# Hybrid encoder on one core: second softmax map in PSUM, query projections beside the first heads, last chunks by token tile

## The chip, the cores and the metric

The kernel runs on one core of one Trainium2 chip. The metric is device time in microseconds for one execution. A core has five engines with a queue of instructions each: TensorE (PE, matmuls, whose weight loads are counted apart as PEld), VectorE (DVE), ScalarE (ACT), GpSimd (POOL) and SyncE (SP), which here issues the DMAs. The engines run side by side and wait for each other by semaphores.

## The reference, cut to what matters

The reference is a bidirectional encoder with two layers on a sequence of 1024 tokens of width 1024, in float32. Each layer projects x to four groups of mixers (a convolution module, an S5 state-space layer, a short gated convolution, differential attention), concatenates the four results, projects them out, normalises, runs a SwiGLU feed-forward network of hidden width 2816 and normalises again. The change touches the attention and the end of the feed-forward network:

```python
def block(q_blk):
    s = jnp.einsum('bqhcd,bkhcd->cbhqk', q_blk, k).astype(jnp.float32)
    p = jax.nn.softmax(s, axis=-1)
    a = p[0] - lam * p[1]
    return jnp.einsum('bhqk,bkhe->bqhe', a.astype(v.dtype), v)

o = lax.map(block, qb).swapaxes(0, 1).reshape(bsz, seq, DA_HEADS, DA_VDIM)
of = of * lax.rsqrt(jnp.mean(of * of, axis=-1, keepdims=True) + LN_EPS)
...
mix = jnp.einsum('bse,ed->bsd', jnp.concatenate([y_a, y_b, y_c, y_d], axis=-1), w_out[l])
x = layer_norm(DEEPNORM_ALPHA * x + mix, ln1_g[l], ln1_b[l])
ff = jax.nn.silu(x @ w_ffn1[l]) * (x @ w_ffn3[l])
x = layer_norm(DEEPNORM_ALPHA * x + ff @ w_ffn2[l], ln2_g[l], ln2_b[l])
```

There are 4 heads with 2 maps each, 8 query blocks of 128 tokens, queries and keys of 32 elements and values of 64. lam is one learned number per layer.

## The kernel before, in words

Float32 matmuls are made of three float32r matmuls on operands split into a high and a low part (`mm3`, lines 554 to 558; `split`, 560).

**Order of the work.** The class `Trunk` describes the computation, but it issues nothing itself: a recorder (`Weaver`, line 112 on) takes down each operation with what it reads and writes. `schedule` (306) then orders all operations of an engine's queue by a list schedule: an operation's priority is its number in the recording plus a shift from the table `SHIFT`, which has an entry for each step and layer (`attn_k0` is step `attn_k` in layer 0); the table `PREF` shifts the choice of engine where an operation can run on more than one (`any2`, `any3`, `anyp`). `emit` (468) issues them. So every instruction of the program carries line 473 in the profile, and is told by the names of its tiles. Large SBUF tiles (`S`, 525) share 11 slots of 16 KB, handed on in the order in which tiles are first used. PSUM has three pools: `g` (line 540) and `b` (543) with two buffers of one bank each, `d` (546) with two buffers of two banks each.

**A layer.** `mixers_in` (1615) streams nine blocks of the input projection through a ring of two weight tiles (`win`), in the order that `in_blocks` (1608) gives; the last three are V, Q and K. `tok_gemm` (645) makes the projection of a pair of token blocks: 48 matmuls 128x256 into a tile `tg` in PSUM. `attn_k` (1256) stores K's projection in `probs` as a buffer, applies rope on POOL, stacks high and low parts (`stg`, on ACT and POOL) and transposes them on PE (`ktp`) into `kst`. `attn_q` (1249) does projection and rope for Q into `vq`. `attn_small` (1198) makes lambda, `load_out` (1368) loads and splits the output weights (`wout`).

**Attention.** `run` (1679) calls `attn_heads` (1293) for each of 8 query blocks j. For each of 4 heads and 2 maps, two matmuls 128x512 write a score tile `sc` (pool `d`), DVE takes the row maximum (into `asm`), ACT computes the exponential into `probs` with its row sum. Then, per head, DVE takes the reciprocals of both sums, scales the second (`asm<-asm,lam`) and combines the two maps (`probs<-probs,asm`). Eight transposes (`atp`) and copies (`aT`) follow, and per pair of heads 32 matmuls `po` with V. After the first pair, `q_stack` (1282) prepares the next block's queries (`qtp`). `attn_finish` (1339) normalises the block's heads and splits the block's four mixer results into `yhl`; `out_half` (1383) and `out_norm` (1395) project out the block before (`wo`) and normalise it in `xr`.

**Feed-forward network.** `token_operands` (1406) prepares the operands, `ffn_up` (1479) makes the two up projections by a scheme of seven products (`up`), whose gated results go to DRAM by way of `gst`. The down projection is again seven products m, each over 11 chunks: `down_prep` (1552) brings a chunk into the rings `aring` and `wring`, `down_unit` (1570) makes three matmuls for each of four token tiles, `down_out` (1578) adds the product into the result `r`. After the products m = 5 and m = 6, `layer_norm` (575) and, in layer 0, `to_xT` (609, transposes `xtp`) finish four token tiles each.

## Time and profile before

| | |
|---|---|
| median of 3 runs | 2503.61 us (2501.72 to 2503.86) |
| the profiled execution | 2499.38 us |
| its span, first to last instruction | 2497.6 us |
| mean granted TensorE clock | 0.961 |
| busy: PE, DVE, POOL, ACT | 92%, 71%, 39%, 32% |

The profiled execution is 1.8 us longer than its span, and 4.2 us shorter than the median. Busy shares are means over the whole program; the windows below give the same by stage. "PEclk" is the clock that TensorE was granted, 1.00 being full speed. A timeline row has the start in us, the duration, the operation with its output and inputs, how many of its kind stand in the row, and in brackets the engine's idle time before it with the operation that ended it. A row of a group has busy time in all, mean duration in ns, and the idle time before its members.

### The profile page before, as it was taken

The page shows a single profiled execution, that of the slowest core. Times are in us where ns is not written, and L with a number is a line of the kernel's source. Part 1 is how long each engine was busy: PE and PEld are TensorE (multiplying, and loading weights), DVE is VectorE, ACT ScalarE, POOL GpSimd, SP SyncE. Part 2 cuts the span into 40 slices and gives each one's busy share as a digit, 9 for nine tenths or more (in the row PEclk, how much of TensorE's full clock was granted, in tenths as well). Part 3 has the DMA queues.
Part 4 walks back from the last instruction along what each step waited for, and adds up shares of the span by engine and source line. Part 5 has one row for each costly group of instructions (what it writes and reads, how often), then busy time and mean ns, then how long its engine had stood idle before and what let it go on. Part 6 is the DMA issues. An engine that isn't in the chain of part 4 may idle for free. (4 is left out here: it accounts for less than half of the span.)

```text
span 2497.6 us, 35091 instructions
## 1 busy us (share of the span) xinstructions
PE 2307.0 (92%) x13300; PEld 1911.4 (77%) x13300; DVE 1785.5 (71%) x2909; ACT 806.2 (32%) x1387; POOL 982.9 (39%) x876
## 2 busy tenths in 40 slices
PE   8999959888999999999989999699989999998996
PEld 7779847666888888778777788477778888886784
DVE  6587578886343443777881975999886777778988
ACT  2412246543222222332334132455433223222220
POOL 2104264535999899433430226444310000002414
PEclk9999959998999999999999999699999999999998
DMA  5223121112232333843332222111223323447332
GB/s 157 71 50 98 31 87 54 56 56 85 81 110 89 118 99 126 310 153 95 118 123 51 62 80 65 60 56 65 77 74 107 117 80 118 152 156 274 93 96 103
DMA packets 213953, 252.92 MB, mean 101 GB/s; under 512 B 57043, under 2 KB 143641, under 8 KB 213529
## 3 DMA queue, kind: packets, MB, share of 16 engines
q1 hardware_dynamic: 213784, 250.67, 31.4%
q8 instruction: 106, 1.74, 0.3%
q14 instruction: 63, 0.51, 0.1%
HBM read 183.82 MB, written 66.81 MB: 100 GB/s over the span
## 5 line engine op out<-in xcount | busy, mean ns | idle before, releaser
L473 PE MATMUL up<-xT,wring 128*128 128x512 f32 x2112 | 486.5, 389 | 1.0 <-POOL wring L473 1.0
L473 PEld LDWEIGHTS up<-xT,wring 128*128 128x128 f32 x2112 | 396.2, 188 | 84.3 <-POOL wring L473 2.1
L473 PE MATMUL dn<-wring,aring 128*128 128x512 f32 x1848 | 432.8, 396 | 25.8 <-DVE aring L473 11.1
L473 PEld LDWEIGHTS dn<-wring,aring 128*128 128x128 f32 x1848 | 351.0, 191 | 105.9 <-DVE aring L473 14.0
L473 PE MATMUL up<-xB,wring 128*128 128x512 f32 x1584 | 368.7, 390 | 0.0
L473 PEld LDWEIGHTS up<-xB,wring 128*128 128x128 f32 x1584 | 298.4, 189 | 62.0
L473 PE MATMUL cg<-xh,win 128*128 128x512 f32 x640 | 209.5, 397 | 4.2 <-DVE conv L473 4.2
L473 PE MATMUL tg<-win,xh 128*128 128x256 f32 x1024 | 194.4, 290 | 1.6 <-ACT s5u L473 0.7
L473 PE MATMUL wo<-wout,yhl 128*128 128x512 f32 x768 | 194.8, 401 | 0.0
L473 ACT ACTIVATE probs<-sc,asm 128x1024 f32<-128x1024 f32 x128 | 143.2, 1120 | 109.2 <-DVE asm L473 103.5
L473 ACT CAST wring<-upraw 128x512 fp32r<-128x512 f32 x164 | 101.9, 621 | 232.0 <-PE up L473 175.9
L473 DVE TENSOR_REDUCE asm<-sc 128x1 f32<-128x1024 f32 x128 | 155.3, 1217 | 25.3 <-PE sc L473 24.9
L473 PEld LDWEIGHTS tg<-win,xh 128*128 128x128 f32 x1024 | 163.6, 196 | 3.6 <-ACT s5u L473 0.9
L473 PEld LDWEIGHTS wo<-wout,yhl 128*128 128x128 f32 x768 | 143.3, 191 | 29.6 <-POOL yhl L473 0.3
L473 DVE TENSOR_TENSOR aring<-araw,aring 128x512 fp32r<-128x512 f32 x152 | 126.9, 842 | 45.8 <-ACT aring L473 42.8
L473 POOL TENSOR_TENSOR upraw<-upraw 128x512 f32<-128x512 f32 x32 | 42.4, 1324 | 292.4 <-ACT wring L473 292.4
L473 POOL TENSOR_TENSOR wring<-upraw,wring 128x512 fp32r<-128x512 f32 x110 | 148.0, 1346 | 6.1 <-ACT wring L473 4.2
L473 PE MATMUL tg<-win,xl 128*128 128x256 f32 x512 | 149.0, 292 | 1.0 <-DVE xl L473 1.0
L473 PEld LDWEIGHTS cg<-xh,win 128*128 128x128 f32 x640 | 120.2, 188 | 31.9 <-DVE conv L473 4.3
L473 ACT CAST aring<-araw 128x512 fp32r<-128x512 f32 x115 | 71.1, 622 | 206.5 <-PE dn L473 168.2
L473 DVE TENSOR_TENSOR tw<-tu,up 128x512 f32<-128x512 f32 x66 | 45.3, 686 | 123.6 <-PE up L473 119.5
L473 PE MATMUL sc<-kst,stg 128*128 128x512 f32 x256 | 96.9, 473 | 31.3 <-ACT probs L473 30.8
(263 smaller groups left out, 3986.4 us busy)
## 6 DMA issues: line engine op xcount, KB each, us to landing
upraw<-in_w_ffn_dram SPq DMA_DIRECT2D x88, 512.0 KB, 3.7
araw<-a_scr SPq DMA_DIRECT2D x154, 256.0 KB, 2.9
a_scr<-gst SPq DMA_DIRECT2D x22, 1536.0 KB, 6.0
...
```

Of the source, the lines that this page charges most:

```text
L473: getattr(e, method)(*args, **kwargs)
```

## The change

Five things are changed.

1. In `attn_heads` the exponentials of a head's second map are written back into the score tile in PSUM; `probs` now has one row per head (four in all) for the first map. Only the second sum's reciprocal is taken per head; its scaling by the first sum and lambda is on POOL; the combination on DVE reads the second map from PSUM. `attn_finish` takes the four other reciprocals at once.
2. The input blocks come in the order V, K, Q. `mixers_in` projects K and the first two token blocks of Q; the other three projections of Q are recorded after the heads of block 0. The tiles `yhl`, `wout` and `xr` are made after them.
3. The operand ring of the down projection is made before the tiles of its weights. In layer 0 this gives it the slot of the second-last `gst` tile in place of that of an up operand (`xB11`); in layer 1 it has the second-last `gst` tile's slot before and after.
4. The last four chunks of the last product (m = 6) are done token tile by token tile, the 12 matmuls of a tile in one go, each tile followed by its sums, its normalisation and, in layer 0, its transposes.
5. All entries of `SHIFT` and `PREF` are new, two of them for example:

```diff
-            "attn_k0": -385, "attn_k1": -165, "attn_q0": 5594, "attn_q1": -532, "attn_small1": 2064,
+            "attn_k0": -598, "attn_k1": 1732, "attn_q0": 484, "attn_q1": -1392, "attn_small0": 5048,
```

The rest of the diff (a class attribute `COMB`, an empty tuple, goes as well):

```diff
@@ -1256,11 +1254,11 @@
     def attn_k(self, xT, w, jp):
         nc = self.nc
         if jp == 0:
-            self.PA = self.S([P, 2, 2, SEQ], F32, "probs")
+            self.PA = self.S([P, 4, SEQ], F32, "probs")
             self.stg = self.S([P, 4, 1024], F32R, "stg")
             self.K = [self.S([P, 4, SEQ], F32R, f"kst{i}") for i in range(2)]
         ps = self.tok_gemm(xT, w, jp)
-        kk = self.PA[:, jp // 2, jp % 2, 0:512].rearrange("p (j n) -> p j n", j=2)
+        kk = self.PA[:, jp, 0:512].rearrange("p (j n) -> p j n", j=2)
         nc.scalar.copy(kk, ps)
         self.rope_pair(kk, jp)
         for i2 in range(2):
@@ -1276,7 +1274,6 @@
 
     def attn_alloc(self):
         self.yhl = self.S([P, 2, 2, KT, P], F32R, "yhl")
-        self.xr = self.S([P, 2, 2, D], F32, "xr")
 
     @step
     def q_stack(self, j):
@@ -1302,7 +1299,8 @@
         for hp in range(2):
             aTs = []
             for h in (2 * hp, 2 * hp + 1):
-                pb = self.PA[:, h % 2]
+                pb = self.PA[:, h]
+
                 for c in range(2):
                     m = 2 * h + c
                     sc = self.d((P, SEQ), "sc")
@@ -1310,20 +1308,16 @@
                         nc.tensor.matmul(sc[:, hf * 512:hf * 512 + 512], lhsT=qst[:, m * P:m * P + P],
                                          rhs=self.K[m // 4][:, m % 4, hf * 512:hf * 512 + 512], start=True, stop=True)
                     v.tensor_reduce(sm[:, m:m + 1], sc, axis=AX.X, op=ALU.max, negate=True)
-                    nc.scalar.activation(pb[:, c, :], sc, AF.Exp, bias=sm[:, m:m + 1], accum_out=sm[:, 8 + m:9 + m])
-                rc = sm[:, 16 + 2 * h:18 + 2 * h]
-                v.reciprocal(rc, sm[:, 8 + 2 * h:10 + 2 * h])
-                v.scalar_tensor_tensor(rc[:, 1:2], rc[:, 1:2], sm[:, 8 + 2 * h:9 + 2 * h], self.neglam, op0=ALU.mult, op1=ALU.mult)
-                if h in self.COMB:
-                    nc.scalar.activation(pb[:, 1, :], pb[:, 1, :], AF.Copy, scale=rc[:, 1:2])
-                    nc.gpsimd.tensor_tensor(pb[:, 0, :], pb[:, 0, :], pb[:, 1, :], op=ALU.add)
-                else:
-                    v.scalar_tensor_tensor(pb[:, 0, :], pb[:, 1, :], rc[:, 1:2], pb[:, 0, :], op0=ALU.mult, op1=ALU.add)
+                    nc.scalar.activation(sc if c else pb, sc, AF.Exp, bias=sm[:, m:m + 1], accum_out=sm[:, 8 + m:9 + m])
+                rc = sm[:, 16 + h:17 + h]
+                v.reciprocal(rc, sm[:, 9 + 2 * h:10 + 2 * h])
+                nc.gpsimd.tensor_scalar(rc, rc, sm[:, 8 + 2 * h:9 + 2 * h], self.neglam, op0=ALU.mult, op1=ALU.mult)
+                v.scalar_tensor_tensor(pb, sc, rc, pb, op0=ALU.mult, op1=ALU.add)
...
@@ -1349,7 +1343,8 @@
         ot = self.b((P, 4, 64), "ot")
         for i in range(2):
             self.tr(ot[:, 2 * i:2 * i + 2, :].rearrange("p h e -> p (h e)"), wf[:, i * P:i * P + P])
-        v.tensor_tensor(w, ot, sm[:, 16:24:2].unsqueeze(2).to_broadcast([P, 4, 64]), op=ALU.mult)
+        v.reciprocal(sm[:, 20:24], sm[:, 8:16:2])
+        v.tensor_tensor(w, ot, sm[:, 20:24].unsqueeze(2).to_broadcast([P, 4, 64]), op=ALU.mult)
@@ -1567,21 +1562,22 @@
         self.split(w(b), sb[:, 0], sb[:, 1])
 
     @step
-    def down_unit(self, n, ps):
-        c = n % (NHID // 2)
-        sa, sb = self.aring[:, n % 4], self.bring[:, n % 4]
-        for i in range(4):
+    def down_unit(self, ns, ps, tiles):
+        for i in tiles:
             s = slice(i * P, i * P + P)
-            self.mm3(ps[i], sa[:, 0, s], sa[:, 1, s], sb[:, 0], sb[:, 1], c == 0, c == NHID // 2 - 1)
-
-    @step
-    def down_out(self, m, ps, r, u):
+            for n in ns:
+                c = n % (NHID // 2)
+                sa, sb = self.aring[:, n % 4], self.bring[:, n % 4]
+                self.mm3(ps[i], sa[:, 0, s], sa[:, 1, s], sb[:, 0], sb[:, 1], c == 0, c == NHID // 2 - 1)
+
+    @step
+    def down_out(self, m, ps, r, u, tiles=range(4)):
 
         nc = self.nc
         v = nc.vector
         add = lambda o, x, y=None: v.tensor_tensor(o, o if y is None else y, x, op=ALU.add)
         axpy = lambda o, x: v.scalar_tensor_tensor(o, o, ALPHA, x, op0=ALU.mult, op1=ALU.add)
-        for i in range(4):
+        for i in tiles:
@@ -1606,7 +1602,7 @@
 
 
     def in_blocks(self):
-        return [OFF_S5, 0, GW, OFF_SC + GW, OFF_SC + 2 * GW, OFF_SC, OFF_DA + 2 * GW, OFF_DA, OFF_DA + GW]
+        return [OFF_S5, 0, GW, OFF_SC + GW, OFF_SC + 2 * GW, OFF_SC, OFF_DA + 2 * GW, OFF_DA + GW, OFF_DA]
 
     def in_ring(self, l):
         self.win = [self.S([P, 2, KT, GW], F32R, "win") for _ in range(2)]
@@ -1672,9 +1668,9 @@
             self.attn_v(xT, w(6), jp)
         nxt(7)
         for jp in range(4):
-            self.attn_q(xT, w(7), jp)
-        for jp in range(4):
-            self.attn_k(xT, w(8), jp)
+            self.attn_k(xT, w(7), jp)
+        self.attn_q(xT, w(8), 0)
+        return w(8)
 
     def run(self):
         nc, t = self.nc, self.t
@@ -1697,15 +1693,19 @@
             self.to_xT(j, x0[j // 4][:, j % 4, :], xT)
         for l in range(DEPTH):
             self.layer = l
-            self.mixers_in(l, xT, yT)
+            wq = self.mixers_in(l, xT, yT)
             self.attn_small(l)
-            self.load_out(l)
-            self.attn_alloc()
             g1, b1 = self.gain_rows(t["ln1_g"], t["ln1_b"], l, "ln1")
             xsrc = xin if l == 0 else x2d
             hls = {}
             for j in range(NJ):
                 sm_o = self.attn_heads(l, j)
+                if j == 0:
+                    for jp in range(1, 4):
+                        self.attn_q(xT, wq, jp)
+                    self.attn_alloc()
+                    self.load_out(l)
+                    self.xr = self.S([P, 2, 2, D], F32, "xr")
                 if 0 < j < NJ - 1:
                     hl = hls.pop(j - 1)
                     self.out_half(j - 1, hl, xsrc, 0)
@@ -1741,9 +1741,9 @@
+            self.aring, self.bring = self.S([P, 4, 2, 512], F32R, "aring"), self.wring
             self.w2_tiles((2, 3, 0, 4, 5))
             r = [self.S([P, 4, D], F32, "r") for _ in range(2)]
-            self.aring, self.bring = self.S([P, 4, 2, 512], F32R, "aring"), self.wring
@@ -1770,7 +1770,17 @@
-                self.down_unit(n, ps)
+                if m == 6 and c >= NC - 4:
+
+                    if c == NC - 1:
+                        for i in range(4):
+                            self.down_unit(range(n - 3, n + 1), ps, (i,))
+                            self.down_out(m, ps, rr, us, (i,))
+                            self.layer_norm(rj(tile_of[i]), g2, b2, (out if l + 1 == DEPTH else x2d)[tile_of[i]], 2)
+                            if l + 1 < DEPTH:
+                                self.to_xT(tile_of[i], rj(tile_of[i]), xT)
+                    continue
+                self.down_unit((n,), ps, range(4))
                 if c == NC - 1:
                     self.down_out(m, ps, rr, us)
                     if m == 4 and l + 1 < DEPTH:
@@ -1778,10 +1788,10 @@
                     if m == 5:
                         if l + 1 < DEPTH:
                             self.in_ring(l + 1)
-                    if m >= 5:
+                    if m == 5:
                         for i in range(4):
-                            j = 4 * (m == 5) + tile_of[i]
-                            self.layer_norm(rj(j), g2, b2, out[j] if l + 1 == DEPTH else x2d[j], 1 + (m == 6))
+                            j = 4 + tile_of[i]
+                            self.layer_norm(rj(j), g2, b2, out[j] if l + 1 == DEPTH else x2d[j])
                             if l + 1 < DEPTH:
                                 self.to_xT(j, rj(j), xT)
 
```

**Where the instructions stand now.** On PE, in the first query blocks of layer 0 (`tg` is a token projection, `win` the weights of Q, `po` and `sc` as above), the order before was:

```order
L473 MATMUL po_310<-aT_313,vq_247 64x128
L473 MATMUL po_310<-aT_318,vq_247 64x128
L473 MATMUL sc_329<-kst_181_265,stg_263 128x512 x2
L473 MATMUL qtp_322<-ident,stg_263 128x128 x4
L473 MATMUL sc_340<-kst_180_264,stg_263 128x512 x2
L473 MATMUL atp_326<-ident,probs_262 128x128 x4
L473 MATMUL atp_327<-ident,probs_262 128x128 x4
L473 MATMUL sc_341<-kst_180_264,stg_263 128x512 x2
L473 MATMUL sc_345<-kst_180_264,stg_263 128x512 x2
L473 MATMUL atp_331<-ident,probs_262 128x128 x4
```

and in the changed kernel the same place, between the heads' matmuls with V and the next scores, reads:

```order
L472 MATMUL tg_313<-win_91,xh_4_87 128x256 x2
L472 MATMUL tg_313<-win_91,xl_6_89 128x256
L472 MATMUL po_290<-aT_298,vq_247 64x128
L472 MATMUL po_290<-aT_293,vq_247 64x128
L472 MATMUL po_290<-aT_298,vq_247 64x128
L472 MATMUL po_290<-aT_293,vq_247 64x128
L472 MATMUL po_290<-aT_298,vq_247 64x128
L472 MATMUL sc_309<-kst_173_257,stg_255 128x512 x2
L472 MATMUL tg_315<-win_91,xh_5_88 128x256 x2
L472 MATMUL tg_315<-win_91,xl_7_90 128x256
```

So before no projection is left among the heads; now the 48 matmuls of `tg_313` end right ahead of `po` of the first pair of heads, those of `tg_315` begin one score tile later, and a third projection follows in the next block.

On DVE in the steady state (block j = 3, first heads; `asm` holds a block's maxima, sums and factors), before:

```order
L473 TENSOR_REDUCE asm_356_440<-sc_359_443 128x1
L473 TENSOR_REDUCE asm_356_440<-sc_363_447 128x1
L473 RECIPROCAL asm_356_440<-asm_356_440 128x2
L473 SCALAR_TENSOR_TENSOR asm_356_440<-asm_356_440,lam_207_291 128x1
L473 SCALAR_TENSOR_TENSOR probs_178_262<-probs_178_262,asm_356_440 128x1024
L473 TENSOR_REDUCE asm_356_440<-sc_364_448 128x1
```

and now:

```order
L472 TENSOR_REDUCE asm_356_440<-sc_359_443 128x1
L472 TENSOR_REDUCE asm_356_440<-sc_363_447 128x1
L472 RECIPROCAL asm_356_440<-asm_356_440 128x1
L472 SCALAR_TENSOR_TENSOR probs_170_254<-sc_359_443,asm_356_440,probs_170_254 128x1024
L472 TENSOR_REDUCE asm_356_440<-sc_364_448 128x1
L472 TENSOR_TENSOR ow_352_436<-ot_354_438,asm_322_406 128x256
L472 TENSOR_REDUCE asm_356_440<-sc_370_454 128x1
```

The scaling by lambda is gone from DVE, the reciprocal is of one value, and the combination has a score tile among its operands. The scaling now stands on POOL, in this order (`xr` and `ln` are the output normalisation, `stg` the stacking of the next queries):

```order
L472 TENSOR_TENSOR xr_332<-xr_332,ln_202_286 128x1024
L472 TENSOR_SCALAR asm_406<-asm_406,lam_285 128x1
L472 TENSOR_TENSOR xr_332<-xr_332,ln_202_286 128x1024
L472 TENSOR_TENSOR stg_255<-vq_247,stg_255 128x8x64
L472 TENSOR_SCALAR asm_440<-asm_440,lam_285 128x1 x2
L472 TENSOR_SCALAR oms_437<-oms_437 128x4
L472 TENSOR_TENSOR oms_437<-oms_437,mhalf 128x4
L472 CAST yhl_319<-yt_435 128x1024
L472 TENSOR_TENSOR yhl_319<-yt_435,yhl_319 128x1024
L472 TENSOR_SCALAR asm_440<-asm_440,lam_285 128x1
```

Three of the four scalings of the block (`asm_440`) are here with the last one of the block before (`asm_406`), between passes over 128x1024 elements.

At the end of the program PE did the last chunks by turns over the four token tiles (`dn_1796` holds two of them, `dn_1797` the others):

```order
L473 MATMUL dn_1712_1796<-wring_1384_1468,aring_1643_1727 128x512 x6
L473 MATMUL dn_1713_1797<-wring_1384_1468,aring_1643_1727 128x512 x6
L473 MATMUL dn_1712_1796<-wring_1384_1468,aring_1643_1727 128x512 x6
L473 MATMUL dn_1713_1797<-wring_1384_1468,aring_1643_1727 128x512 x6
L473 MATMUL dn_1712_1796<-wring_1384_1468,aring_1643_1727 128x512 x6
L473 MATMUL dn_1713_1797<-wring_1384_1468,aring_1643_1727 128x512 x6
```

and now:

```order
L472 MATMUL dn_1712_1796<-wring_1384_1468,aring_1636_1720 128x512 x6
L472 MATMUL dn_1713_1797<-wring_1384_1468,aring_1636_1720 128x512 x6
L472 MATMUL dn_1712_1796<-wring_1384_1468,aring_1636_1720 128x512 x6
L472 MATMUL dn_1713_1797<-wring_1384_1468,aring_1636_1720 128x512 x6
L472 MATMUL dn_1712_1796<-wring_1384_1468,aring_1636_1720 128x512 x12
L472 MATMUL dn_1713_1797<-wring_1384_1468,aring_1636_1720 128x512 x6
L472 MATMUL dn_1712_1796<-wring_1384_1468,aring_1636_1720 128x512 x12
L472 MATMUL dn_1713_1797<-wring_1384_1468,aring_1636_1720 128x512 x18
```

The last matmuls are now those of one pair of tiles; the other pair's are done ahead of them.

## Rows read from the trace of the kernel before

**Rows 1.** The page: its first line, busy time of each engine
```profile
span 2497.6 us, 35091 instructions
PE 2307.0 (92%) x13300; PEld 1911.4 (77%) x13300; DVE 1785.5 (71%) x2909; ACT 806.2 (32%) x1387; POOL 982.9 (39%) x876
```

**Rows 2.** Windows of layer 0: stage of K, blocks 0 and 1, steady blocks
```profile
core 0: us, PE busy (x) PEld busy (x) DVE busy (x) ACT busy (x) POOL busy (x), PEclk, DMA share, GB/s
297.90:335.10 37.20, 19.77 (x105) 13.38 (x103) 20.31 (x35) 16.97 (x27) 29.19 (x45) 0.72 0.15 52
335.10:384.10 49.00, 36.03 (x203) 25.68 (x203) 36.45 (x44) 29.08 (x51) 29.71 (x18) 0.66 0.26 86
384.10:554.90 170.80, 151.88 (x1047) 121.93 (x1045) 145.81 (x185) 96.88 (x173) 76.19 (x58) 0.98 0.17 56
```

**Rows 3.** Windows, layer 1: the same three stages
```profile
1546.00:1573.00 27.00, 15.04 (x112) 13.13 (x110) 24.68 (x30) 7.76 (x12) 24.69 (x23) 0.70 0.35 117
1573.00:1621.50 48.50, 31.31 (x205) 22.42 (x204) 44.88 (x62) 26.08 (x46) 16.52 (x12) 0.71 0.15 51
1621.50:1780.00 158.50, 150.97 (x1069) 122.09 (x1068) 148.56 (x208) 82.98 (x150) 71.68 (x60) 1.00 0.18 59
```

**Rows 4.** Timeline of PE, stage of K: start, us, operation, idle before
```profile
330.10 1.32 PE L473 MATMUL ktp<-ident,stg 128*128 128x128 f32 x8 [5.28 <-DVE lam L473]
```

**Rows 5.** Timeline of PE, layer 1: a token projection at full clock
```profile
1529.10 0.40 PE L473 MATMUL tg<-win,xh 128*128 128x256 f32 x2
1529.46 0.40 PE L473 MATMUL tg<-win,xh 128*128 128x256 f32 x2
```

**Rows 6.** Groups by form, 400 to 550 us: busy, mean ns, idle
```profile
L473 DVE TENSOR_REDUCE asm<-sc 128x1 f32<-128x1024 f32 x42 | 51.1, 1217 | 11.5 <-PE sc L473 11.5
L473 ACT ACTIVATE probs<-sc,asm 128x1024 f32<-128x1024 f32 x44 | 49.3, 1121 | 29.0 <-DVE asm L473 29.0
L473 DVE SCALAR_TENSOR_TENSOR probs<-probs,asm 128x1024 f32<-128x1024 f32 x22 | 39.2, 1782 | 0.6
L473 DVE SCALAR_TENSOR_TENSOR asm<-asm,lam 128x1 f32<-128x1 f32 x21 | 12.7, 603 | 0.6
L473 DVE SCALAR_TENSOR_TENSOR xr<-xr,wo 128x512 f32<-128x512 f32 x11 | 7.4, 677 | 3.6 <-PE wo L473 3.6
L473 POOL TENSOR_SCALAR oms<-oms 128x4 f32<-128x4 f32 x5 | 1.0, 193 | 50.6 <-DVE oms L473 50.6
L473 POOL TENSOR_TENSOR xr<-xr,ln 128x1024 f32<-128x1024 f32 x11 | 26.2, 2386 | 8.6 <-ACT xr L473 8.2
```

**Rows 7.** Timeline of DVE: the same combination beside POOL's pass, and without one
```profile
411.56 3.49 DVE L473 SCALAR_TENSOR_TENSOR probs<-probs,asm 128x1024 f32<-128x1024 f32 x1
418.58 1.28 DVE L473 SCALAR_TENSOR_TENSOR probs<-probs,asm 128x1024 f32<-128x1024 f32 x1
```

**Rows 8.** Timeline of POOL: the passes beside the first of them
```profile
409.10 4.86 POOL L473 TENSOR_TENSOR xr<-xr,ln 128x1024 f32<-128x1024 f32 x2 [1.36 <-ACT xr L473]
```

**Rows 9.** Timeline of PE, layer 0: the second FFN half begins
```profile
1068.60 3.78 PE L473 MATMUL dn<-wring,aring 128*128 128x512 f32 x14 [1.49 <-ACT aring L473]
```

**Rows 10.** Timeline of PE: from layer 0 to layer 1
```profile
1263.58 1.09 PE L473 MATMUL xtp<-ident,r 128*128 128x128 f32 x8 [2.08 <-POOL r L473]
1266.94 1.94 PE L473 MATMUL xtp<-ident,r 128*128 128x128 f32 x8 [2.26 <-issue]
```

**Rows 11.** Timeline of PE: the last matmuls of the program
```profile
2471.05 7.13 PE L473 MATMUL dn<-wring,aring 128*128 128x512 f32 x23 [2.18 <-DVE wring L473]
```

**Rows 12.** Timeline of DVE: the tail of the program
```profile
2473.44 2.48 DVE L473 TENSOR_TENSOR r<-r,ln 128x1024 f32<-128x1024 f32 x2 [1.02 <-POOL r L473]
2493.21 1.41 DVE L473 SCALAR_TENSOR_TENSOR r<-r,rs,ln 128x512 f32<-128x512 f32 x2 [0.46 <-POOL rs L473]
```

**Rows 13.** Windows, layer 0: two blocks, one at full clock and one not
```profile
415.20:442.50 27.30, 24.22 (x172) 19.40 (x173) 23.96 (x31) 16.27 (x29) 13.52 (x11) 1.00 0.23 72
442.50:471.40 28.90, 25.77 (x173) 20.54 (x174) 24.05 (x31) 16.27 (x29) 13.61 (x11) 0.94 0.22 70
```

7 lines of the change are left out of this document (3 added, 4 removed), and 69 rows, old and new, of tables (PREF, SHIFT).

## The prediction

> **What bounds the kernel now.** I read the page first, then windows by stage, then the timelines of the stages that the change touches. TensorE is busy 92% of the 2497.6 us span [rows 1], so no edit can be worth more than the 190 us in which it stands, and only edits in stages where it stands count. The windows say where that is. Attention is not one stage but three. [...] Layer 1 has the same three: 12.0 us idle of 27.0, 17.2 of 48.5, and only 7.5 of 158.5 [rows 3]. [...]
>
> In the stage of K, TensorE waits for a chain over ScalarE, GpSimd and VectorE; its longest stand is 5.28 us [rows 4]. In a steady block of 27.3 us neither engine is full (TensorE 24.22, VectorE 23.96, [rows 13]). What stops them is one long instruction: the combination of the two maps, alone 1.28 us, took 3.49 us beside two passes of GpSimd that ended at 413.96, 1.1 us before it did at 415.05 [rows 7, 8]. So it ran only once GpSimd was done. Its mean in this stage is 1782 ns, and the tiny scaling ahead of it has a mean of 603 ns [rows 6].
>
> **The change, part by part.** The profiled execution took 2499.38 us, 4.2 us under the median of 2503.61; the sum is made against the profiled time, and the 4.2 us are added at the end.
>
> *Three query blocks beside the first heads, layer 0.* A projection of two token blocks is 48 matmuls; three of them take 0.36 us at full clock [rows 5], so it costs 16 x 0.36 = 5.76 us. Before, all four of Q (23.0 us) stood ahead of K's. Now K's come first, Q's first one goes behind them, beside the chain that TensorE waits for, and the other three (17.3 us) go into the first two blocks. What leaves the front is at most 23.0 us, if the first one fits into the 17.4 us in which TensorE stands in K's stage. What comes back lies in blocks 0 and 1, which have 13.0 us of idle time: nothing if all of it is filled and the higher clock shortens the 36.03 us beside it; 34.6 - 13.0 = 21.6 us if the three run at half clock and fill just the holes. With the first projection uncovered as well that is between -23 and +4. I take a lengthening of 8 us, so **-15**: nearer the good end, because the 0.66 itself follows from the holes that are being filled. GpSimd's ropes for those three leave the stretch ahead of K's too, and come back beside heads that keep it busy 29.71 of 49 us [rows 2]. The loads of the output weights, the yhl and xr tiles now wait until Q's operands are free. The first output projection stood at the end of block 1, at 384.06 us, so those loads have two blocks to hide in; if they did not, the first output projection would be late, not the heads.
>
> *Layer 1.* The same with less to win: there the projections already stand among K's transposes, and K's stage has 12.0 us idle, not 17.4 [rows 3]. At best -17.3; at half clock 34.6 - 17.2 = 17.4 come back, so 0, and a few us worse if K's stage is late (+4). I take **-10**.
>
> *Second exponentials kept in PSUM, in the six steady blocks.* VectorE reads the second map from PSUM. This form with a 128x1024 operand is not in the trace; the nearest row, half as long, with one operand in PSUM, took 677 ns [rows 6], so 1.35 us. The lower bound is 1.28, that of the undisturbed form; the upper is the present mean, 1.78. Taking 1.35, because the mean of that half-long form leaves no room for stretched ones, VectorE loses 4 x (1.78 - 1.35) + 4 x 0.60 = 4.1 us a block and drops to about 20. GpSimd gains four scalings; the nearest row is 193 ns [rows 6], 0.8 us a block, nothing on an engine under half full. TensorE's 24.2 us then bind. All its idle time in this stage is 18.9 us in layer 0 and 7.5 in layer 1; these are the best cases, and 0 the worst that this part gives without a new wait (that is the third rival). I take **-8** and **-3**, less than half, since each head now has one more handover, from VectorE to GpSimd and back, and since a second-map score buffer is held longer: reduction 1.22, exponential 1.12, then also scaling 0.19 and combination 1.35, together 3.9 us instead of 2.3. There are two such buffers and 6.8 us per head, so it fits, but not with much to spare.
>
> The single reciprocals for the output (one of four values a block) cost about as much as the half of each head's reciprocal that goes: nothing.
>
> *Operand ring first.* In layer 0 the ring gets a slot that is free earlier; TensorE waits 1.49 us for an operand early in the second half [rows 9]. Between 0 and -1.5: **-1**. In layer 1 the ring keeps its kind of slot: 0.
>
> *Last chunks by token tile.* At the end of layer 0 TensorE stands 2.08 and 2.26 us around the first transposes of the result [rows 10]. Finishing one token tile some 24 matmuls ahead of the end lets its normalisation run beside the others' matmuls. All of it gone is -4.3; by the same measure, VectorE taking a gain row first would cost 2: **-3**. At the end of the program the last matmul ends at 2478.2 [rows 11] and VectorE's last work at 2494.6 [rows 12]. The first tile's sums are ready up to 7 us earlier (23 matmuls take 7.13 us there), but VectorE is busy with two gain rows until 2475.9 [rows 12], and in the order of the change these two still stand among tile 0's operations; VectorE's tail is its own work, one thing after the other. Between +2 and -7: **-2**.
>
> *The order tables* move everything a little. In the up halves TensorE has no holes to lose, and I cost them at nothing.
>
> Sum: -15 - 10 - 8 - 3 - 1 - 3 - 2 = **-42**; 2499.4 - 42 = 2457.4, and against the median 2461.6 us.
>
> **Rivals.**
>
> *A: the clock dips in each block.* Where a score buffer is held longer, TensorE may pause briefly before each score. One block in the trace already had a granted clock of 0.94 and took 28.9 us, against 27.3 at 1.00 [rows 13]: 1.6 us. In the twelve steady blocks that is 19 us: 2461.6 + 19 = 2481. For it: buffers held 3.9 us instead of 2.3. Against: layer 1's steady blocks, just as dense, are at 1.00 [rows 3]. [...]
>
> *B: the query blocks are not hidden.* They run at half clock between scores and lengthen the first blocks by what they save: the two start terms come to nothing, 2461.6 + 25 = 2487. For it: 0.66 and 0.71 in just these blocks [rows 2, 3]. Against: the holes filled are the cause of that clock.
>
> *C, the other side: the scaling waits on GpSimd.* Its 0.2 us stand in GpSimd's queue behind passes over xr of 2386 ns [rows 6], one of which itself waits for a normalisation; the combination behind it waits on VectorE, and everything behind that (reductions of the next scores, copies of transposes) with it. The gain of 42 us is eaten at 42 / 64 = 0.66 us of uncovered wait per head. With half a pass, 1.2 us, for each of 64 heads it is +77: 2539, slower. For it: in the new order nearly every scaling stands directly behind such a pass, and the present VectorE stretch (1.78 against 1.28) is the same collision in another place. Against: GpSimd is busy only 13.5 of 27.3 us [rows 13], and the combination is late today by up to 2.2 us already.
>
> *D: it does nothing.* The planner puts things so that what it wins in attention it loses elsewhere by the new tables: within 5 us of 2503.6.
>
> **Chances.** Forecast 0.55, A 0.12, B 0.14, C 0.15, D 0.04. The low end of the range is both start terms at their best (15 more) and both steady terms at theirs (15 more): 2432. The high end holds A, B and most of both at once (2506): 2500. Left out are C and little else. About 0.2%, 5 us, is what a measurement of this kernel can tell from no change. Faster by more than that: the forecast, A and nearly all of B, 0.80; the same: D and a rest of B, 0.05; slower: C, 0.15.
>
> **What would show it.** Right: no `tg` of Q ahead of K's, blocks 0 and 1 at a clock over 0.8 and under 57 us long; in steady blocks the combination near 1.35 us with no 3.5 us among them, VectorE near 20 us of some 26, TensorE over 24; the first transposes of the result beside the last `dn`. Wrong: VectorE idle ahead of the combination for GpSimd (C), a clock under 0.95 in most steady blocks (A), blocks 0 and 1 over 65 us (B), or TensorE waiting in FFN stages where it did not before (D).

## The result, and the profile after

| | before | after |
|---|---|---|
| median | 2503.74 us (4 runs) | 2458.94 us (4 runs, 2457.63 to 2462.01) |
| profiled execution's span | 2497.6 us | 2460.1 us |
| mean granted clock | 0.961 | 0.961 |

The ratio is 0.9821 (95% interval 0.9806 to 0.9836): faster by 44.8 us, where 42 were forecast, well inside the range of 2432 to 2500. The sum was right; most of its terms were not. The two profiled executions differ by 37.4 us (2499.38 and 2462.01), less than the medians, since the first is 4.4 us under its median and the second 3.1 us above. The stages below account for the spans of these two. The page of the changed kernel begins:

```profile
span 2460.1 us, 35076 instructions
PE 2298.1 (93%) x13300; PEld 1913.1 (78%) x13300; DVE 1758.8 (71%) x2905; ACT 793.7 (32%) x1348; POOL 951.0 (39%) x935
```

TensorE is busy 8.9 us less than before [rows 1] and the span is 37.5 us shorter, so 28.6 us are idle time. To see where, I cut both spans at the same landmarks of TensorE's timeline: the end of the last convolution projection (`cg`), the first score, the last matmul `po`, the first and last `up`, the last `dn`. Where a single query block is given, it is counted from its first row maximum on VectorE to that of the next. The columns that follow the change are runs of the experiments below; idle time of TensorE stands in brackets.

| us | before | after | heads undone, own tables | Q ahead, own tables | Q ahead, mixed tables |
|---|---|---|---|---|---|
| layer 0: start to last cg | 209.8 (18.8) | 214.8 (24.4) | 204.4 (17.7) | 219.4 (26.6) | 204.7 (17.6) |
| to first score | 125.3 (17.4) | 106.2 (13.3) | 102.0 (11.7) | 110.5 (6.3) | 109.2 (5.3) |
| to last po | 224.1 (31.7) | 218.7 (17.5) | 226.0 (21.9) | 202.8 (20.4) | 200.4 (17.5) |
| to first up | 50.9 | 47.3 | 48.0 | 48.2 | 50.9 |
| up | 421.4 | 419.2 | 419.2 | 420.1 | 419.2 |
| to last dn | 230.0 (10.2) | 230.7 (13.7) | 241.4 (20.6) | 237.7 (16.8) | 226.3 (10.1) |
| layer 1: to first tg | 7.2 | 9.0 | 7.7 | 9.6 | 14.6 |
| to last cg | 184.0 | 180.3 | 184.7 | 185.9 | 185.4 |
| to first score | 120.4 (13.5) | 103.5 (11.0) | 102.6 (12.0) | 111.6 (6.9) | 109.2 (4.2) |
| to last po | 208.4 (23.8) | 218.6 (18.9) | 218.5 (16.8) | 199.4 (16.4) | 200.9 (17.7) |
| to first up | 45.8 | 47.9 | 45.3 | 47.7 | 44.4 |
| up | 420.8 | 421.1 | 420.7 | 422.1 | 419.9 |
| to last dn | 230.2 (15.5) | 220.7 (5.6) | 224.5 (8.4) | 223.1 (7.9) | 220.1 (6.7) |
| to the end | 19.4 | 22.1 | 22.2 | 22.1 | 22.1 |

Attention is where most of it went, but not as forecast. Windows of the changed kernel, layer 0's blocks 0 and 1 and a steady block, then a hole and a steady block of layer 1 (columns as in [rows 2]):

```profile
core 0: us, PE busy (x) PEld busy (x) DVE busy (x) ACT busy (x) POOL busy (x), PEclk, DMA share, GB/s
321.00:357.00 36.00, 26.65 (x166) 22.32 (x166) 22.83 (x26) 15.38 (x25) 11.37 (x15) 0.71 0.07 20
357.00:387.00 30.00, 22.70 (x174) 18.78 (x175) 19.87 (x25) 16.18 (x29) 23.10 (x29) 0.83 0.33 113
...
411.70:435.80 24.10, 23.93 (x173) 19.57 (x172) 19.98 (x29) 16.13 (x29) 13.01 (x15) 1.00 0.25 82
...
1576.00:1597.00 21.00, 11.35 (x82) 9.48 (x80) 12.10 (x17) 4.30 (x8) 5.56 (x10) 0.67 0.34 118
1641.50:1665.60 24.10, 23.92 (x174) 19.73 (x173) 21.20 (x30) 15.17 (x28) 12.90 (x15) 1.00 0.26 83
```

A steady block takes 24.1 us, with TensorE busy 23.9 of them at full clock: TensorE binds, as the prediction had it, and nearly all the idle time of [rows 2] and [rows 13] is gone: from block 2 of layer 0 to the last `po` it was 18.9 us and is 0.9 us. Blocks 0 and 1 of layer 0, though, take 66 us from the first score on, not 49, and still have 16.7 us of holes at clocks of 0.71 and 0.83. The query projections came in addition to the holes, not into them, as TensorE's rows show:

```profile
326.70 1.22 PE L472 MATMUL sc<-kst,stg 128*128 128x512 f32 x2 [3.60 <-ACT probs L472]
330.43 1.97 PE L472 MATMUL atp<-ident,probs 128*128 128x128 f32 x8 [2.51 <-DVE probs L472]
...
336.97 1.22 PE L472 MATMUL sc<-kst,stg 128*128 128x512 f32 x2 [2.86 <-ACT probs L472]
...
343.40 0.40 PE L472 MATMUL tg<-win,xh 128*128 128x256 f32 x2
...
343.76 0.40 PE L472 MATMUL tg<-win,xh 128*128 128x256 f32 x2
...
378.84 0.69 PE L472 MATMUL otp<-ident,ow 128*128 128x128 f32 x2 [4.20 <-DVE ow L472]
```

In block 0 TensorE waits 8.97 us for exponentials and a combination, all of it ahead of the first projection. The projections (`tg`) then stand in lumps of 48, two in block 0 and one in block 1, at 0.36 us for three, the full-clock price of [rows 5]. The wait of 4.20 us for `ow` in block 1 is explained in run 8 below.

The groups of the heads:

```profile
L472 DVE SCALAR_TENSOR_TENSOR probs<-sc,asm,probs 128x1024 f32<-128x1024 f32 x64 | 81.8, 1279 | 16.9 <-POOL asm L472 16.8
L472 PE MATMUL atp<-ident,probs 128*128 128x128 f32 x512 | 78.8, 290 | 4.3 <-DVE probs L472 3.8 <-ACT aT L472 0.5
L472 POOL TENSOR_SCALAR asm<-asm,lam 128x1 f32<-128x1 f32 x64 | 30.3, 473 | 142.6 <-DVE asm L472 134.2 <-DVE lam L472 8.2
```

The combination takes 1279 ns in the mean, where it was 1600 before over the whole trace and 1782 in the steady blocks [rows 6]. None of the 64 is longer than 1.29 us; before, 9 took over 2 us. Before, the 30 that ran with no GpSimd instruction beside them took at most 1.29 us, the other 34 took 1.88 us in the mean and up to 3.50. Now 42 of the 64 have one beside them, and none is stretched. One such place, VectorE first, then GpSimd:

```profile
437.47 1.28 DVE L472 SCALAR_TENSOR_TENSOR probs<-sc,asm,probs 128x1024 f32<-128x1024 f32 x1 [0.42 <-POOL asm L472]
```

```profile
437.10 0.34 POOL L472 TENSOR_SCALAR asm<-asm,lam 128x1 f32<-128x1 f32 x1
437.39 2.39 POOL L472 TENSOR_TENSOR xr<-xr,ln 128x1024 f32<-128x1024 f32 x1
```

Nearly all of the combination lies inside a pass of 2.39 us, and it takes 1.28 us, as if alone; the same pair before was [rows 7, 8]. The small scaling (here 0.34 us) holds the combination up by 0.42 us at this place, 16.8 us over all 64.

The ring and the ends, by four rows of TensorE and VectorE: the new wait in layer 0's `dn`, the transposes between the layers (2.08 and 2.26 us before, [rows 10]), the last matmuls and the last operation of VectorE:

```profile
1037.94 6.99 PE L472 MATMUL dn<-wring,aring 128*128 128x512 f32 x22 [7.05 <-DVE aring L472]
...
1241.40 1.97 PE L472 MATMUL xtp<-ident,r 128*128 128x128 f32 x8 [4.46 <-POOL r L472]
...
2424.68 13.36 PE L472 MATMUL dn<-wring,aring 128*128 128x512 f32 x57
```

```profile
2455.74 1.41 DVE L472 SCALAR_TENSOR_TENSOR r<-r,rs,ln 128x512 f32<-128x512 f32 x2 [0.46 <-POOL rs L472]
```

The last 57 matmuls now run without a stand (there was one of 2.18 us [rows 11]), but VectorE still works 19.1 us after them (2438.0 to 2457.2), where it was 16.4 before [rows 11, 12].

### The profile page after: what moved, and what is told of

The parts are those of the page before. It is cut to its first block, busy times and chain, and to the rows that moved or that the text cites. A ratio compares the mean times of both kernels' runs of the same rounds, so it can differ in the third digit from the quotient of the medians.

```text
span 2460.1 us, 35076 instructions
## 1 busy us (share of the span) xinstructions
PE 2298.1 (93%) x13300; PEld 1913.1 (78%) x13300; DVE 1758.8 (71%) x2905; ACT 793.7 (32%) x1348; POOL 951.0 (39%) x935
## 4 chain that ended last, share of the span: by engine, by line
PE 70%; DVE 15%; DMA 5%; POOL 5%; ACT 3%; issue 2%; SPq 0%; POOLq 0%; DVEq 0%; ACTq 0%
PE up L472 32%; PE dn L472 13%; PE tg L472 5%; PE wo L472 5%; PE cg L472 4%; DVE s5k L472 3%; DMA w<-in_w_ffn_dram 2%; PE sc L472 2%; PE po L472 2%; PE atp L472 2%; DVE s5t L472 1%; DVE s5w L472 1%; ACT convz L472 1%; POOL rs L472 1%; DVE r L472 1%
## 5 line engine op out<-in xcount | busy, mean ns | idle before, releaser
L472 PE MATMUL dn<-wring,aring 128*128 128x512 f32 x1848 | 430.0, 394 | 16.8 <-DVE aring L472 11.4
L472 ACT CAST wring<-upraw 128x512 fp32r<-128x512 f32 x134 | 83.2, 622 | 320.0 <-PE up L472 256.1
L472 POOL TENSOR_TENSOR wring<-upraw,wring 128x512 fp32r<-128x512 f32 x111 | 154.6, 1394 | 47.9 <-ACT wring L472 47.7
L472 ACT CAST aring<-araw 128x512 fp32r<-128x512 f32 x126 | 77.8, 622 | 214.0 <-PE dn L472 176.6
L472 POOL CAST wring<-upraw 128x512 fp32r<-128x512 f32 x72 | 48.4, 672 | 219.0 <-PE up L472 184.6
L472 DVE TENSOR_TENSOR wring<-w,wring 128x512 fp32r<-128x512 f32 x154 | 119.5, 777 | 8.6 <-ACT wring L472 7.9
L472 PE MATMUL cg<-xl,win 128*128 128x512 f32 x320 | 125.3, 391 | 0.0
```

What stands on the lines that cost most here:

```text
L472: getattr(e, method)(*args, **kwargs)
```

## The experiments

The kernel before took 2496 to 2498 us in the experiments and 2504 beside the change, so I compare ratios to the kernel before of the same chip, and stages by the traces.

**1. The heads of the kernel before in the changed kernel.**

```diff
-    nc.scalar.activation(sc if c else pb, sc, AF.Exp, ...)
+    nc.scalar.activation(pb[:, c, :], sc, AF.Exp, ...)
-    nc.gpsimd.tensor_scalar(rc, rc, ...)
+    v.scalar_tensor_tensor(rc[:, 1:2], rc[:, 1:2], ...)
-    v.scalar_tensor_tensor(pb, sc, rc, pb, op0=ALU.mult, op1=ALU.add)
+    v.scalar_tensor_tensor(pb[:, 0, :], pb[:, 1, :], rc[:, 1:2], pb[:, 0, :], op0=ALU.mult, op1=ALU.add)
```

> The changed kernel with the heads of the kernel before (second map's exponentials in SBUF, both reciprocals and the scaling on VectorE), all else as changed, the new tables too. Theory 'PSUM operand': the changed kernel's steady blocks of 24.1 us come from the combination no longer standing behind GpSimd; undone, the combination is stretched again (mean 1.5 us or more, some rows of 3.5) and the steady blocks go back to 26 to 29 us: 2475 to 2491 us. Rival 'order': the new tables alone give the 24.1 us; steady blocks stay under 25 us and the time under 2466.

Measured 0.9948 (0.9932 to 0.9965), 2484.98 us. Steady blocks of layer 0 took 26.4 us, the combination 1549 ns:

```profile
L472 DVE SCALAR_TENSOR_TENSOR probs<-probs,asm 128x1024 f32<-128x1024 f32 x64 | 99.1, 1549 | 1.2
```

It agrees with "PSUM operand", but the planner made a new order for this kernel with tables that were not made for it, so some of the 2.3 us a block may be that.

**2. The new heads alone in the kernel before**, the same lines the other way round.

> The kernel before with the heads of the change alone, old tables, old place of Q. 'PSUM operand': steady blocks fall to 24 to 25 us in both layers, 18 to 32 us less than before: 2472 to 2486 us. Rival 'order': 2498 us or more, the combination short but TensorE still waiting as often.

Measured 0.9977 (0.9963 to 0.9991), 2493.44 us: neither. The combination was 1279 ns as in the change, yet steady blocks took 23.9 to 27.6 us and VectorE waited 25.7 us for GpSimd's scalings:

```profile
L473 DVE SCALAR_TENSOR_TENSOR probs<-sc,asm,probs 128x1024 f32<-128x1024 f32 x64 | 81.9, 1279 | 26.5 <-POOL asm L473 25.7
```

Blocks 2 to 6 of layer 0 and 3 to 6 of layer 1 together took 229.6 us, in the kernel before 240.9: 11.3 us less. The edit shortens the instruction in every order that was run (a mean of 1.28 us in the eleven traces with the new heads, 1.50 to 1.60 in the three with the old ones). How much the block gains depends on the order.

**3. The small scaling back on VectorE.**

```diff
-                nc.gpsimd.tensor_scalar(rc, rc, sm[:, 8 + 2 * h:9 + 2 * h], self.neglam, op0=ALU.mult, op1=ALU.mult)
+                v.scalar_tensor_tensor(rc, rc, sm[:, 8 + 2 * h:9 + 2 * h], self.neglam, op0=ALU.mult, op1=ALU.mult)
```

> The changed kernel with the small scaling back on VectorE. 'Handover costs little': VectorE takes up to 4 x 0.6 us a block more and saves 0.26 us of waiting for GpSimd per head; TensorE binds at 24.1 us a block either way, 2454 to 2464 us. Rival 'the scaling must leave VectorE': it stands behind GpSimd's passes again (some rows over 1 us) and blocks grow by 1 us or more: 2470 us or more. Rival 'the handover costs': under 2452 us.

Measured 0.9948 (0.993 to 0.9966), 2485.25 us: my theory missed by 20 us, and the signs of the first rival were all there. 15 of the 64 scalings took over 0.7 us, the longest 2.70. The group of the scaling and a steady block:

```profile
L472 DVE SCALAR_TENSOR_TENSOR asm<-asm,lam 128x1 f32<-128x1 f32 x64 | 35.8, 560 | 1.0
```

```profile
434.50:459.90 25.40, 24.15 (x174) 19.75 (x173) 22.55 (x34) 16.15 (x29) 11.74 (x11) 1.00 0.25 79
```

The block is 1.3 us longer, but VectorE still is not full. So the engine, the form of the instruction or the new order is to blame. The next run keeps the order.

**4. The same, in the changed kernel's own order.** The planner still counts the scaling as GpSimd's; only when it is issued it goes to VectorE, so every engine keeps its order. It also keeps the form that it has on GpSimd, `tensor_scalar`; run 3 had `scalar_tensor_tensor`.

```diff
                 e = getattr(self.nc, o.eng)
+                if o.eng == "gpsimd" and str(o.grp).startswith("attn_heads") and o.calls[0][0] == "tensor_scalar":
+                    e = self.nc.vector
```

> The changed kernel with its own order of instructions kept on every engine; only the 64 small scalings are issued to VectorE instead of GpSimd, at the same place. This tells apart what the scaling's engine costs and what a new plan costs, since putting the scaling back on VectorE with a new plan cost 25 us. Theory 'new plan': in the same order VectorE has room, blocks stay at 24.1 to 24.4 us, 0.980 to 0.985 of the kernel before. Rival 'scaling on VectorE is the cost': blocks grow to 25.3 us or more as in that run, 0.990 to 0.996.

Measured 0.9832 (0.9812 to 0.9852), 2457.25 us: no different from the change. The scalings and a steady block:

```profile
L474 DVE TENSOR_SCALAR asm<-asm,lam 128x1 f32<-128x1 f32 x64 | 16.9, 265 | 0.7
L474 DVE SCALAR_TENSOR_TENSOR probs<-sc,asm,probs 128x1024 f32<-128x1024 f32 x64 | 81.9, 1280 | 1.8
```

```profile
431.80:455.80 24.00, 23.89 (x174) 19.58 (x173) 20.76 (x34) 16.14 (x29) 11.76 (x11) 1.00 0.26 84
```

In this form and order the engine of the scaling is worth nothing. The scalings took 241 to 275 ns here, those beside a GpSimd instruction too, where run 3's form took 0.20 to 0.22 us with none beside it and up to 2.70 us beside one. So of the 24.6 us by which run 3 had the longer span (2484.7 against 2460.1), the 18.0 us in attention can be the new order or the form, which no run separates. The other 6.6 us lie in stages without a scaling, which only the order reaches. (Where the order is the same, as in this run and the changed kernel, the stages outside attention differ by up to 1.2 us from trace to trace.) An edit in this kernel is badly priced by leaving it out while the planner is free and its tables are another kernel's.

**5. All of Q ahead of the heads.**

```diff
-        self.attn_q(xT, w(8), 0)
+        for jp in range(4):
+            self.attn_q(xT, w(8), jp)
...
-                    for jp in range(1, 4):
-                        self.attn_q(xT, wq, jp)
```

> The changed kernel with all four query projections behind K's and ahead of the heads; the loads of the output weights stay behind the heads of block 0. In the changed kernel the stretch ahead of the first score lost 17 to 19 us per layer and blocks 0 and 1 grew by as much. Theory 'moved, not hidden': equal, 2454 to 2464 us. Rival 'hidden beside the heads': 2475 us or more, 17 us per layer. Rival 'the chain of K hides them better': blocks 0 and 1 shrink by 17 us per layer and the stretch ahead grows by less than 10: 2437 to 2450 us.

Measured 0.9961 (0.9944 to 0.9978), 2488.52 us. By the number alone the place beside the heads is worth 1.4%, as its rival has it. But in layer 0 the stretch ahead of the first score grew by 18.4 us and the heads lost 14.5, nearly equal. In layer 1 it grew by 21.1 and the heads lost only 2.5: blocks 0 to 2 lost 12.2, while the later ones, which hold no projection in either kernel, grew by 9.7. Inconclusive: here too the order is new, under tables made for another kernel.

**6. The old tables in the changed kernel.**

> The changed kernel with the tables of the kernel before. Theory 'parts need their plan': with the old tables the steady blocks are 25 to 28 us, as with the heads alone, and the Q projections lie worse: 0.990 to 1.005 of the kernel before. Rival 'the edits carry it': under 0.985, steady blocks at 24 to 25 us.

Measured 1.0055 (1.0035 to 1.0075), 2512.87 us: slower than the kernel before, a little past the upper end expected. All edits without their tables lose; the tables are worth 2.3% of this change. Steady blocks took 24.6 to 26.3 us. The blocks summed in run 2 took 229.1 us, 11.8 less than before, and with the new tables, in the changed kernel, 217.7.

**7. The end undone:** the last four chunks in turn for all token tiles.

```diff
-                if m == 6 and c >= NC - 4:
...
-                    continue
-                if m == 5:
+                if m >= 5:
```

> The changed kernel with the last chunks of the last product done for all four token tiles in turn, as before. The prediction gave the tile-wise end -3 and -2 us; the trace of the change shows the end of layer 0 1.8 us and the tail of the program 2.7 us longer than before. Theory 'the tile-wise end wins nothing': from last dn to the end 19 to 20 us instead of 22.1, layer 0's end as before, 0 to 4 us less in all (other stages aside). Rival 'the end won and VectorE's other work hid it': both ends get longer than in the changed kernel by 3 us or more.

Measured 0.9855 (0.9836 to 0.9875), 2463.10 us, which the intervals don't tell from the change. Its stages do: from the last `up` of layer 1 to the end it took 245.1 us, the changed kernel 242.8; from the last `up` of layer 0 to the first `tg` 238.6 against 239.7. So under the new tables the tile-wise end wins about 2 us at the end of the program and nothing at the end of layer 0 (1 us longer), which is neither the theory nor the rival. Under the old tables (run 6, with the tile-wise end) the two stretches took 250.8 and 239.0 us, in the kernel before 249.6 and 237.2: no gain shows there at all. That the tail is longer than before comes with the new tables: it is 23.1 us here too, and was 18.5 us with the old tables in run 6.

**8. Two of Q's projections behind the finish of block 0.** In layer 1 the window 1576 to 1597 above holds 9.65 us in which TensorE stood. TensorE, ScalarE, GpSimd:

```profile
1582.86 0.69 PE L472 MATMUL ot<-ident,ow 128*128 128x128 f32 x2 [4.81 <-ACT ow L472]
1588.39 0.69 PE L472 MATMUL otp<-ident,ow 128*128 128x128 f32 x2 [4.84 <-DVE ow L472]
```

```profile
1582.43 0.37 ACT L472 COPY ow<-po 128x256 f32<-128x256 f32 x1 [3.23 <-POOL vq L472]
```

```profile
1580.82 1.57 POOL L472 TENSOR_TENSOR vq<-ropet 128x64 f32<-128x64 f32 x2
```

ScalarE's copy of the head sums into `ow` began 0.04 us after GpSimd's last rope ended. The rope's intermediate values (`ropet`) and `ow` have one tag with one buffer, so block 0's finish waits for the last rope of Q, which the change put ahead of it; and the transposes of `ow` stand on TensorE ahead of those of block 1.

```diff
-                    for jp in range(1, 4):
-                        self.attn_q(xT, wq, jp)
+                    self.attn_q(xT, wq, 1)
...
                 hls[j] = self.attn_finish(l, j, yT, *sm_o)
+                if j == 0:
+                    self.attn_q(xT, wq, 2)
+                    self.attn_q(xT, wq, 3)
```

(The loads of the output weights and xr follow them.)

> The changed kernel with the second and third moved query projection and the loads of the output weights recorded behind the finish of block 0. The ropes and the head finish share one small buffer (one tag, one buffer), and in layer 1 the finish of block 0 waited for the last rope, with TensorE standing 4.81 and 4.84 us behind it; in layer 0 4.2 us. Theory 'shared buffer': these three stands go, blocks 0 to 2 of layer 1 shorten by 8 us or more. Rival 'late weights': the stands stay or move, since the loads of the output weights wait for the same projections.

Measured 0.9891 (0.9867 to 0.9914), 2470.94 us. Layer 1's blocks 0 to 2 took 80.7 us, not 91.7, and of the two stands one of 2.19 us was left: as the theory has it. Layer 0's stand went from 4.20 to 2.47 us. But under the new order layer 0's blocks 2 to 4 went to 28 and 29 us and layer 1's blocks 3 to 6 from 96.5 to 104.2 us, so it is slower in all.

**9. to 11. Three edits with tables made for them.** To compare edits fairly, SHIFT and PREF were searched anew for each, with the planner's own estimate as the measure. By that estimate nothing better was found for the kernel before or for the change. No run tests this, and the estimate is a weak guide: layer 0 up to the last `cg`, which none of these edits touches, took 204.4 us with one set of tables and 219.4 with another (table above).

Run 9, the heads undone as in run 1:

> The changed kernel with the heads of the kernel before, as in the first of these runs, but now with SHIFT and PREF tables made for it, so that it isn't held back by tables that fit another kernel. Theory 'PSUM operand': the combination still stands behind GpSimd (mean 1.5 us or more), which no order removes: steady blocks 25.5 us or more, 0.986 to 0.996 of the kernel before. Rival 'the plan was all': 24 to 24.5 us a block and 0.984 or less.

Measured 0.9897 (0.988 to 0.9913), 2470.24 us. The groups of the combination and the scaling, and two steady blocks:

```profile
L475 DVE SCALAR_TENSOR_TENSOR probs<-probs,asm 128x1024 f32<-128x1024 f32 x64 | 96.2, 1504 | 1.3
L475 DVE SCALAR_TENSOR_TENSOR asm<-asm,lam 128x1 f32<-128x1 f32 x64 | 26.6, 416 | 0.9
```

```profile
392.70:418.10 25.40, 24.51 (x172) 19.29 (x170) 23.05 (x33) 15.89 (x29) 12.70 (x10) 1.00 0.22 75
418.10:443.90 25.80, 24.44 (x177) 19.83 (x176) 23.26 (x33) 15.70 (x29) 13.34 (x10) 1.00 0.25 80
```

The long ones are still there (7 of 64 over 2 us), and steady blocks are 25.4 and 25.8 us with TensorE busy 24.5. In blocks 2 to 6 of layer 0 and 3 to 6 of layer 1 the kernel before took 137.1 and 103.8 us, this one 128.5 and 100.6, the changed kernel 121.2 and 96.5. So of 23.2 us won there, 11.8 go with the order and the other edits and 11.3 with the heads, 1.3 us a block. Runs 2 and 6 gave the same halves from the other side. In attention as a whole less of it is left: from the last `cg` to the last `po` this kernel took 649.1 us in the two layers, the changed kernel 647.0, because up to the start of block 2 this one was 15.1 us shorter, with Q in the same place. The other differences to the change lie in stages that the edit doesn't touch (`dn` of layer 0 10.7 us longer, the first stretch 10.4 shorter).

Run 10, all of Q ahead as in run 5:

> The changed kernel with all query projections ahead of the heads and tables made for that. With the changed kernel's tables this was 0.996. Theory 'moved, not hidden': what blocks 0 and 1 grow by beside the projections is what the stretch ahead of them saves; with fitting tables 0.978 to 0.985. Rival 'hidden beside the heads': the place is worth 10 us or more, 0.987 to 0.996.

Measured 0.9862 (0.9848 to 0.9877), 2462.04 us: between the ranges of the theory and the rival. The stretch ahead of the first score grew by 4.3 and 8.1 us and the heads lost 15.9 and 19.2, so neither's account holds. In attention, from the last `cg` to the last `po`, it took 313.3 and 311.0 us, the changed kernel 324.9 and 322.1: 11 us less per layer. It lost as much in stages that the edit does not touch (table above, up to the last `cg` and in `dn`).

Run 11, the ropes' values in the xr tile, not in the shared buffer (xr is now made ahead of the heads, and the loads of the output weights stand behind the finish of block 0):

```diff
+        tt = self.xr[:, 0, 1, 256 * jp:256 * jp + 256].rearrange("p (a j m e) -> p a j m e", a=4, j=2, m=8) if jp else None
-        self.rope_pair(qq, jp)
+        self.rope_pair(qq, jp, tt)
```

> The changed kernel in which the ropes of the three moved query projections use a piece of the xr tile for their intermediate values, not the one buffer that they share with the head finish; xr is made first and the output weights are loaded behind the finish of block 0; tables made for it. Theory 'shared buffer': the stands of 4.8 and 4.8 us in layer 1 and 4.2 us in layer 0 go, blocks 0 to 2 shorten by 8 us or more in layer 1, 0.974 to 0.980. Rival 'late elsewhere': they wait for the next thing, 0.981 or more.

Measured 0.9849 (0.9834 to 0.9864), 2459.00 us. The transposes of `ow` over the whole trace, first of the changed kernel, then of this one:

```profile
L472 PE MATMUL otp<-ident,ow 128*128 128x128 f32 x32 | 7.2, 313 | 12.2 <-DVE ow L472 12.1
L472 PE MATMUL ot<-ident,ow 128*128 128x128 f32 x32 | 6.5, 286 | 5.1 <-ACT ow L472 5.1
```

```profile
L475 PE MATMUL otp<-ident,ow 128*128 128x128 f32 x32 | 6.6, 288 | 6.1 <-DVE ow L475 6.0
L475 PE MATMUL ot<-ident,ow 128*128 128x128 f32 x32 | 6.1, 274 | 0.5 <-ACT ow L475 0.5
```

The stands in front of them fell from 17.3 to 6.6 us, and blocks 0 to 2 of layer 1 from 91.7 to 78.4 us; but two of that layer's next four take 28.5 and 27.1 us. In all it is no faster than the change: the theory holds where the buffer is, its number went to the rival. Blocks 0 and 1 of layer 0 in this run:

```profile
319.50:340.40 20.90, 13.54 (x69) 9.60 (x69) 14.15 (x19) 11.76 (x19) 1.09 (x4) 0.65 0.00 0
340.40:370.40 30.00, 29.90 (x270) 28.35 (x269) 26.37 (x31) 16.99 (x31) 14.97 (x24) 1.00 0.06 19
```

All 144 matmuls of the three projections stand in block 1, where TensorE is busy 29.9 of 30.0 us at full clock; in the kernel before that block took 28.4 us with 8.2 us idle. Block 0, which holds none of them, keeps 7.4 us of holes. Up to the start of block 2 this run took 154.5 and 155.4 us in the two layers, 19.3 and 12.9 less than the kernel before. All of attention took 627.8 us, the changed kernel 647.0. Most of that was lost again ahead of attention, in stages that the edit doesn't touch (217.9 and 191.5 us up to the last `cg`, in the changed kernel 214.8 and 180.3).

**12. Q ahead, with the tables of the steps outside attention from the runs in which those stages were shortest.**

> All query projections behind K's and ahead of the heads, as in the run before with tables made for that, but with the tables of the steps outside attention taken from those runs in which their stages were shortest (the stretch up to the last convolution projection of layer 0 was 204.4 us long in the run of the undone heads with its own tables, 214.8 us in the changed kernel and 219.3 us in the run of the query projections ahead with its own tables). In that last run attention took 313.3 and 311.0 us from the last convolution projection to the last matmul with V, in the changed kernel 324.9 and 322.1. Theory 'the place beside the heads costs, a fitting plan pays': both gains add up, 10 us at least in the first stretch and 20 us in attention: 0.965 to 0.975 of the kernel before, about 0.010 under the changed kernel's 0.982. Rival 'what one stage wins another loses': 0.980 or more, as in the runs so far.

Measured 0.9728 (0.9705 to 0.9751), 2429.05 us: both gains add up, and it is about 0.9% faster than the changed kernel. Of the 33.0 us between the two spans, 10.1 lie in the first stretch, which the place of Q doesn't touch. The changed kernel or run 11 with mixed tables was not run. Its page, then windows of the stretch up to the first score, blocks 0 and 1, and a steady block:

```profile
span 2427.1 us, 35114 instructions
PE 2280.3 (94%) x13300; PEld 1900.7 (78%) x13300; DVE 1736.3 (72%) x2879; ACT 795.6 (33%) x1369; POOL 936.7 (39%) x940
```

```profile
216.10:314.30 98.20, 92.92 (x764) 86.56 (x764) 71.59 (x149) 35.60 (x66) 40.51 (x62) 0.97 0.24 74
317.90:364.50 46.60, 31.03 (x203) 24.16 (x204) 37.52 (x48) 27.09 (x48) 8.62 (x14) 0.74 0.11 37
411.40:435.20 23.80, 23.80 (x174) 19.81 (x173) 20.21 (x30) 14.93 (x27) 14.30 (x16) 1.00 0.27 84
```

With three more projections behind K's, TensorE is busy 92.9 of 98.2 us there at a clock of 0.97; blocks 0 and 1 are back at 46.6 us, with 15.6 us of holes (13.0 before, [rows 2]).

## Why the prediction was right, and where its steps were not

The forecast's direction, size and binding engine were right. By its own steps, against the spans of the two traces (37.5 us):

- **The query blocks, -15 and -10: failed.** Up to the start of block 2 it is 173.8 us before and 172.1 after in layer 0, 168.4 and 170.3 in layer 1. Together that is nothing, as rival B had it, and B's sign is there: blocks 0 and 1 take 65.9 and 66.7 us at clocks of 0.76 and 0.77. B's reason is not, since the projections ran at full clock (0.36 us for three matmuls). The step that failed is "a lengthening of 8 us ... because the 0.66 itself follows from the holes that are being filled". That the holes set the clock was my inference; the traces show the two together. Before, the clock was 0.51 from 313.9 to 351.9 us, with TensorE busy 19.70 of 38.00 us, and 1.00 in the next 6 us, with 4.24 busy; in the changed kernel 0.50 from 313.9 to 341.9 (14.76 of 28.00) and 1.00 from 341.9 to 371.9 (27.55 of 30.00), where all three projections of layer 0 lie. In my upper ends a projection takes twice as long at half clock; no projection of Q ran at that clock in these two traces. A score matmul took 628 ns in the median from 314 to 350 us before, and 398 from 384 to 442 at 1.00. Blocks 0 and 1 grew by 17.4 and 18.7 us, and kept 16.7 and 18.0 us of idle time (13.0 and 17.2 before). In layer 0 the holes ahead of the first lump are waits for the chain of scores, maxima and exponentials, and the projections were put behind them. Another 4.20 us in layer 0 and 9.65 in layer 1 came from a buffer that I had not looked for: I had asked who waits for the moved projections' operands, not which buffers their ropes use. The forecast was within reach all the same: run 11, with that buffer freed and other tables, won 19.3 and 12.9 us up to block 2. How much of this is the buffer and how much the order stays open, since run 11 changed both; run 9, with the old heads, the buffer still shared and other tables, won 10.4 and 4.5 us there. Open too is whether the place beside the heads or the one behind K's projection is better: all of attention took 627.8 us in run 11, 624.3 in run 10 and 619.7 in run 12, each with other tables. Behind K the projections do cover K's chain (5.3 us idle in run 12, 13.3 in the changed kernel, 17.4 before).
- **The heads, -8 and -3: right mechanism, too small.** From block 2 to the last `po` it is 175.6 us before and 152.8 after in layer 0 (-22.8), 160.4 and 151.8 in layer 1 (-8.6). Both are past the ends that I had given (-19, -7.5). In layer 0 those ends held the idle time but not the dips of the clock: a block at 0.94 [rows 13] has none now (1.00 over the 152.8 us). In layer 1 the clock was at 1.00 before and after; why TensorE's busy time fell there too, by 2.0 us, is open. I had taken less than half for the handover to GpSimd and the longer held score buffer. The handover costs nothing that shows (2457.25 us without it in run 4, 2458.94 with it), the buffer neither (steady blocks have 0.2 us idle). The reciprocals took 158 ns for two values before and 157 for one after, so no time is saved there, and the sixteen of four values add 2.6 us on VectorE in all. By runs 2, 6 and 9 half of the gain in the steady blocks is the heads' edit, 11.3 us, which is close to the 11 forecast. The other half is the order's, which I had put at nothing.
- **The ring, -1:** 230.0 and 230.7 us for `dn` in layer 0, no difference that two traces can show. One new wait of 7.05 us for an operand stands there now, a sign that I had named for rival D; `dn` of layer 1 lost 9.9 us of idle time instead. The ring was not tried by itself.
- **The ends, -3 and -2:** run 7 gives about +1 and -2 under the new tables, and under the old ones no gain shows. In the trace both are longer (+1.8 and +2.7), the second with the tables.
- **The tables, 0: failed.** They make the difference between 1.0055 and 0.982 (run 6). In `dn` of layer 1 the time fell by 9.5 us; with all the edits under the old tables it was 232.3 us, more than before, so this is theirs. From layer 1's first `tg` to its last `cg`, which no other edit touches, they gave 3.7, and at the start they cost 5.0. I had read the order tables as moving everything "a little", though the rows that I quoted were the work of such tables themselves.

So the number came out because the 25 us that did not come in the first blocks were nearly made up by 20 more in the later ones, and because all other stages together gave 6.4 us where 6 had been forecast, for other reasons. That these errors cancel is luck.

Rival A did not occur: the granted clock from block 2 to the last `po` is 1.00 in both layers of the changed kernel. Rival C did not occur either: the scaling is held up by 0.26 us a head, under the 0.66 at which it would decide.
